# A matrix difference held behind the splits of a three-block sum on VectorE, in the feed-forward of a one-core encoder layer

## The chip, the cores and the metric

The kernel runs on one core of a Trainium2 chip. The metric is the device time of one execution in microseconds (us), the median of the runs. Lower is better.

## The reference

One layer of a hybrid encoder (256 frames, model width 2048, feed-forward width 5632), all in float32. The change lies in the feed-forward; what stands before it (three mixers, gates, an output projection) is left as it is.

```
    h2 = rms_norm(x, g_ffn)
    gate, up = jnp.split(h2 @ w_ffn_in, 2, axis=-1)
    return x + (jax.nn.silu(gate) * up) @ w_ffn_out
```

A final RMSNorm follows. `w_ffn_in` is 2048 x 11264, `w_ffn_out` 5632 x 2048.

## The kernel before, in words

**Products in halves.** TensorE multiplies numbers of a short form (fp32r). So each float32 matrix is split into an upper half (`whi`, ScalarE copies with rounding) and a lower half (`wlo`, VectorE subtracts the upper half from the original), and a product takes three matmul passes: upper by upper, upper by lower, lower by upper. The weights come from memory in float32 and every piece of them, 128 x 1024, is split on the chip: a ScalarE copy (L733) and a VectorE subtraction (L734) for each piece.

**Groups and fewer products.** The gate and up columns are worked off in 22 groups, 256 columns of each per group. A group has four weight blocks of 128 x 2048 (1 MiB each): B11 and B21 (the gate block for the two halves of the model width), X and B22 (the up block likewise). Groups 0 and 1 are plain, with eight block products for a 2 x 2 by 2 x 2 product. Groups 2 to 21 use a scheme with seven products, for which sums of blocks are formed on the chip:

- X arrives as B12 + B22: SyncE loads B12 into X's tile (L765), then a DMA that adds in place, issued by GpSimd (`load_sum`, L769), adds B22 to it.
- `q2` (L877): VectorE adds B11 to X. X is now the three-block sum.
- `q4` (L888): a DMA that adds in place, issued by GpSimd, adds X to B21.
- `q1` (L891): VectorE forms X - B22, which is B11 + B12, into B11's tile. The change is about this difference.

**Pieces.** Every product has two pieces (halves of the block), and the pieces of all groups stand in one list, `line`. In a late group g it reads: X with form 4 (two pieces), a piece of output weights, the sum with form 5 (two), B21 with form 1 (two), output, the difference with form 3 (two), B11 of group g + 1 with form 0 (two), output, B22 with form 6 (two), B21 + X with form 2 (two), output. The output pieces are the second feed-forward matrix for the chunk of groups before it (`down`, 24 matmuls on L115 to L117; a piece of a group has 12, on L792). `run` goes through the list: for each piece it emits the matmuls, and it splits three pieces ahead (`LOOK`), in `split_piece`. A piece has functions to be called before its split (`pre`), after it (`done`) and after its matmuls (`post`). There are four tiles each for upper and lower halves.

**Tiles and loads.** Seven tiles of 1 MiB (`raws`) hold the weights. `Weights` counts the pieces that still use a tile; when the last has been split, the tile goes back and `fill` loads the next block of `todo` into it. `todo` is sorted by the first piece that uses a block (X eight pieces earlier). SyncE issues the plain loads, one after the other: a load that waits for its tile holds up those behind it. GpSimd issues the additions, also in order. Within an engine, the order is set by a scheduler that goes by priorities and dependences; `tc.issue_after` adds a dependence.

**Lines.** The names and lines that matter here: `Piece` (L701), `fill` (L717), `split_piece` (L724), `Group` (L762), `product` (L785), `group` (L874) with `q2`, `q4`, `q1`, and `down` (L938), whose loads are on L945. `turn` (L923) transposes a group's result on TensorE (L931); its four transposes stand behind the sum's product of each group.

Of the kernel before, what the change touches and what calls it, by code (L numbers as in the profile page):

```python
# [7 lines left out]
F32 = mybir.dt.float32  # L8
# [38 lines left out]
def block_kernel(ctx: ExitStack, tc: tile.TileContext, xT, vec,  # L47
                 wvf, wqk, wxy, wpi, wgate, wri, wpool, wbr, wout, wffi, wffo, out):
    nc = tc.nc
    V, S, G, PE = nc.vector, nc.scalar, nc.gpsimd, nc.tensor  # L50
# [8 lines left out]
    class InOrder:  # L59


        def __init__(self, engine):
            self.engine, self.last = engine, None
# [24 lines left out]
    def split(r, a, n, V=V, S=S):  # L88

        hi = hl_p.tile([P, RAW // 2], F32R, name="whi")  # L90
        lo = hl_p.tile([P, RAW // 2], F32R, name="wlo")
        with tc.high_priority(offset=AHEAD):
            S.copy(hi[:, :n], r[:, a:a + n])  # L93
            V.tensor_sub(lo[:, :n], r[:, a:a + n], hi[:, :n].bitcast(F32))  # L94
        return hi, lo
# [207 lines left out]
    def split_w(k):  # L303
        return split(raws[k // 2], k % 2 * W3, W3, Vo, So)
# [14 lines left out]
    for k in range(EARLY):  # L319
# [7 lines left out]
        else:  # L327
            w = split_w(k)
# [13 lines left out]
    w = ahead  # L342
# [12 lines left out]
    for k in range(EARLY, KD):  # L355
# [13 lines left out]
        w = ahead  # L369
# [31 lines left out]
    def scores(h, q, k):  # L401

        sc = aux()
        for t in range(2):
            n = (t + 1) * P
            o = sc[:, off[t]:off[t] + n]
            tq = slice(t * P, (t + 1) * P)
            tl = slice(T + t * P, T + (t + 1) * P)
            PE.matmul(o, lhsT=q[:, tq], rhs=k[:, :n], start=True, stop=False)
            PE.matmul(o, lhsT=q[:, tq], rhs=k[:, T:T + n], start=False, stop=False)  # L410
            PE.matmul(o, lhsT=q[:, tl], rhs=k[:, :n], start=False, stop=False)
            PE.matmul(o, lhsT=LF[:, h, tq], rhs=RF[:, h, :n], start=False, stop=True)
        ns = at_p.tile([P, 3 * P], F32, name="ns")
        st = at_p.tile([P, 8], F32, name="st")
        ph = at_p.tile([P, 3 * P], F32R, name="ph")
        pl = at_p.tile([P, 3 * P], F32R, name="pl")
        for t in range(2):
            c = slice(off[t], off[t] + (t + 1) * P)
            V.tensor_tensor_reduce(out=ns[:, c], in0=sc[:, c], in1=mask[:, c], scale=-1.0,
                                   scalar=3e38, op0=ALU.add, op1=ALU.min, accum_out=st[:, t:t + 1])  # L420
            S.activation(ns[:, c], ns[:, c], AF.Exp, bias=st[:, t:t + 1], scale=-1.0,
                         accum_out=st[:, 2 + t:3 + t])
        V.reciprocal(st[:, 4:6], st[:, 2:4])
        for t in range(2):
            c = slice(off[t], off[t] + (t + 1) * P)
            S.activation(ph[:, c], ns[:, c], AF.Copy, scale=st[:, 4 + t:5 + t])
            V.scalar_tensor_tensor(pl[:, c], ns[:, c], st[:, 4 + t:5 + t], ph[:, c].bitcast(F32),
                                   ALU.mult, ALU.subtract)
        return ph, pl
# [47 lines left out]
    for h in range(H):  # L477
# [3 lines left out]
        p = scores(h, q, k)  # L481
# [157 lines left out]
    for m in range(KD):  # L639
# [3 lines left out]
        for b, y in enumerate((yB, yC, yA)):  # L643
            hi, lo = split(r3, b * 1024, 1024) if b < 2 else split(r1, 0, 1024)
# [56 lines left out]
    class Piece:  # L701
# [3 lines left out]
        def __init__(self, src, mm, uses, pre=(), done=(), post=()):  # L705
            self.src, self.mm, self.uses = src, mm, uses
            self.pre, self.done, self.post = list(pre), list(done), list(post)
            for w in uses:
                w.uses += 1
                if w.first is None:  # L710
                    w.first = len(line)
                    todo.append(w)
            line.append(self)

    line, todo = [], []

    def fill():  # L717

        while raws and todo:
            w = todo.pop(0)  # L720
            w.tile = raws.pop(0)
            w.load(w.tile)

    def split_piece(p, ahead):  # L724
        for f in p.pre:
            f()
        hi = hl_p.tile([P, RAW // 2], F32R, name="whi")[:, :1024]
        lo = hl_p.tile([P, RAW // 2], F32R, name="wlo")[:, :1024]
        w = p.src()
        if len(w.shape) == 3:  # L730
            hi, lo = halves(hi), halves(lo)
        with tc.high_priority(offset=ahead):
            S.copy(hi, w)  # L733
            V.tensor_sub(lo, w, hi.bitcast(F32))  # L734
        for f in p.done:
            f()
        for w in p.uses:
            w.uses -= 1
            if not w.uses:
                raws.append(w.tile)  # L740
        fill()
        p.parts = hi, lo

    def run():

        n = 0
        for i, p in enumerate(line):
            while n < len(line) and n <= i + LOOK:
                split_piece(line[n], AHEAD if n <= LOOK else 0)
                n += 1  # L750
            p.mm(*p.parts)
            for f in p.post:
                f()

    def halves(r):
        return r.rearrange("p (j c) -> p j c", j=2)
# [28 lines left out]
    def product(g, w, form, c, start, pre=None, done=None, post=None, more=()):  # L785

        for h in range(2):
            def mm(hi, lo, h=h):
                o = g.place(c)
                for part, v in ((0, hi), (1, hi), (0, lo)):  # L790
                    for j in range(4):
                        PE.matmul(o, lhsT=hs[:, 4 * h + j, form, part, :], rhs=v[:, :, j * P:(j + 1) * P],  # L792
                                  start=start and h == 0 and part == 0 and v is hi and j == 0,
                                  stop=h == 1 and v is lo and j == 3, skip_group_check=True)

            Piece(lambda h=h: halves(w.tile)[:, :, h * 512:(h + 1) * 512], mm, [w, *more],
                  [pre] if pre and h == 0 else [], [done] if done and h else [],
                  [post] if post and h else [])

    def tmp(nm):  # L800
        return ft_p.tile([P, T], F32, name=nm)

    def gated(t, a, up, g):

        V.scalar_tensor_tensor(a, up, r2[:, t:t + 1], g, ALU.mult, ALU.mult)
# [4 lines left out]
    def first(g):  # L810
        if g.i in PLAIN:
            both(g, g.b11, (("C", 4, True), ("A", 0, True)), lambda: less(g, "t0", "A", "C"))
        else:
            product(g, g.b11, 0, "A", True, post=lambda: copy(g, "m1", "A"))
# [59 lines left out]
    def group(g, nxt, slot, mid):  # L874

        def q2():
            V.tensor_add(g.x.tile, g.x.tile, g.b11.tile)  # L877

        def d():
            g.d = sm.tile([P, T], F32, name="t0")  # L880
            V.tensor_sub(g.d, g.m1, g.bank["B"])

        def silu0():
            g.g0 = sm.tile([P, T], F32, name="t1")
            S.activation(g.g0, g.bank["A"], AF.Silu, scale=r2[:, 0:1])

        def q4():
            G.dma_start(g.b21.tile, g.x.tile, accum_op=ALU.add)  # L888

        def q1():  # L890
            V.tensor_sub(g.b11.tile, g.x.tile, g.b22.tile)  # L891

        def s():
            s_ = sm.tile([P, T], F32, name="evt")
            V.tensor_sub(s_, g.bank["B"], g.m1)
            g.u1 = tmp("u1")
            V.tensor_sub(g.u1, s_, g.bank["C"])

        def up0():
            V.tensor_sub(g.m1, g.bank["B"], g.m1)  # L900
            gated(0, g.m1, g.m1, g.g0)

        def end():
            V.tensor_add(g.d, g.d, g.bank["C"])
            S.activation(g.d, g.d, AF.Silu, scale=r2[:, 1:2])
            gated(1, g.u1, g.u1, g.d)

        product(g, g.x, 4, "C", True)
        slot(0)

        product(g, g.x, 5, "B", True, pre=q2, post=d, more=[g.b11])
        mid()
        product(g, g.b21, 1, "A", False, done=q4, post=silu0, more=[g.x])
        slot(1)
        product(g, g.b11, 3, "B", False, pre=q1, post=s, more=[g.x, g.b22])
        if nxt is not None:
            first(nxt)
        slot(2)
        product(g, g.b22, 6, "B", False, post=up0)
        product(g, g.b21, 2, "C", False, post=end)  # L920
        slot(3)
# [71 lines left out]
    for i, (c, at) in enumerate(owner):  # L993
        g, prev = nxt, (g if i else None)
        nxt = Group(i + 1) if i + 1 < len(owner) else None

        def slot(k):
            if nxt is None and k == 3:
                return
            for _ in range(SLOTS[c][k]):  # L1000
                if queue:
                    queue.pop(0)()

        def mid():
            if prev is None:
                behind(stats)
                return
            pc, pat = owner[i - 1]
            behind(lambda a=(prev, pc, 2 * pat): turn(*a))
            if pc != c:  # L1010
                queue.extend(down(pc))
# [147 lines left out]
```

## Time and profile before

| | |
|---|---|
| median of 3 runs | 1530.01 us (1529.73 to 1530.49) |
| the profiled execution | 1532.99 us, its span 1531.0 us |
| TensorE (PE) busy | 1508.2 us, 99% |
| TensorE weight loads (PEld) busy | 1411.3 us, 92% |
| VectorE (DVE) busy | 1205.4 us, 79% |
| ScalarE (ACT) busy | 923.8 us, 60% |
| GpSimd (POOL) busy | 119.5 us, 8% |
| feed-forward | from about 800 us to the end |

The profile is of one execution. The shares are averages over the whole span, and the stages differ much. Times in the rows are in us from the span's start. A row of the timeline merges neighbouring instructions of one kind: start, length of the stretch, engine, line, operation, out<-in, shape, count, and in brackets the idle time before it and what ended it. An SPq row is a DMA's issue on SyncE; POOL rows with DMA_DIRECT2D are issues on GpSimd. Both say nothing of the landing, which is given apart.

### The profile page before, as it was taken

How to read it: one execution, taken by the hardware profiler on the slowest of the kernel's cores; microseconds unless marked ns; L12 is line 12 of the kernel's file. 1: busy time of each engine (PE TensorE's matmuls, PEld its weight loads, DVE VectorE, ACT ScalarE, POOL GpSimd, SP SyncE). 2: the span in 40 equal slices, each digit the busy share in tenths (PEclk: the TensorE clock that was granted, in tenths of full speed). 3: DMA queues.
4: the chain of work that ended last, by engine and by line, in shares of the span. 5: the costliest groups of instructions: out<-in, count | busy, mean ns of one | idle time of the engine just before them, and what ended most of it. 6: DMA issues, size and time to landing. Idle time of an engine off the chain costs nothing.

```text
span 1531.0 us, 26475 instructions
## 1 busy us (share of the span) xinstructions
PE 1508.2 (99%) x10628; PEld 1411.3 (92%) x10628; DVE 1205.4 (79%) x1593; ACT 923.8 (60%) x1319; POOL 119.5 (8%) x170
## 2 busy tenths in 40 slices
PE   9999999999999999999999999999999999999996
PEld 8988888888888888888889999999999999999996
DVE  7866677788565656567796999999889998999974
ACT  6766567666454444455675666566565665656663
POOL 1000011202000000000110010010000000000012
PEclk9999999999999999999999999999999999999998
DMA  7644455555555554656757699878889888887851
GB/s 259 212 165 150 135 192 185 200 173 206 189 183 199 172 207 165 206 170 234 264 187 219 197 254 277 286 228 252 258 275 295 243 249 267 281 278 242 238 204 55
DMA packets 70858, 331.09 MB, mean 216 GB/s; under 512 B 5584, under 2 KB 6480, under 8 KB 52816
## 3 DMA queue, kind: packets, MB, share of 16 engines
q1 hardware_dynamic: 61840, 286.54, 52.3%
q0 software_dynamic: 8320, 41.95, 14.5%
q8 instruction: 83, 1.36, 0.3%
q10 hardware_dynamic: 576, 0.92, 0.2%
q14 instruction: 39, 0.32, 0.1%
HBM read 306.32 MB, written 2.10 MB: 201 GB/s over the span
## 4 chain that ended last, share of the span: by engine, by line
PE 90%; DVE 4%; DMA 2%; issue 1%; ACT 1%; POOL 0%; SPq 0%; POOLq 0%; DVEq 0%; ACTq 0%
PE acc L106 30%; PE bank L792 23%; PE acc L107 15%; PE obank L117 5%; PE obank L116 5%; PE obank L115 5%; PE bank L834 3%; DVE wlo L734 2%; DMA raw<-raw 2%; PE acc L72 1%; PE aux L72 1%; PE turn L931 1%; DMA raw<-in_wvf 1%; DVE wlo L72 0%; POOL lev L580 0%
## 5 line engine op out<-in xcount | busy, mean ns | idle before, releaser
L733 ACT CAST whi<-raw 128x1024 fp32r<-128x1024 f32 x384 | 393.9, 1050 | 226.9 <-PE obank L116 57.5
L734 DVE TENSOR_TENSOR wlo<-raw,whi 128x1024 fp32r<-128x1024 f32 x384 | 456.4, 1220 | 61.5 <-ACT whi L733 59.0
L106 PE MATMUL acc<-hT,whi 128*128 128x512 f32 x1392 | 489.7, 395 | 0.0
L94 DVE TENSOR_TENSOR wlo<-raw,whi 128x1024 fp32r<-128x1024 f32 (+1 forms) x262 | 320.2, 1222 | 188.9 <-ACT whi L93 188.2
L93 ACT CAST whi<-raw 128x1024 fp32r<-128x1024 f32 (+1 forms) x262 | 270.2, 1032 | 208.5 <-PE acc L106 181.6
L107 PE MATMUL acc<-hT,wlo 128*128 128x256 f32 x1392 | 390.7, 281 | 0.0
L106 PEld LDWEIGHTS acc<-hT,whi 128*128 128x128 f32 x1392 | 261.6, 188 | 59.4
L792 PE MATMUL bank<-whi,hs 128*128 128x256 f32 x2240 | 312.6, 281 | 1.5 <-ACT whi L733 1.5
L792 PEld LDWEIGHTS bank<-whi,hs 128*128 128x128 f32 x2240 | 284.0, 188 | 2.4 <-ACT whi L733 2.1
L107 PEld LDWEIGHTS acc<-hT,wlo 128*128 128x128 f32 x1392 | 262.4, 189 | 0.0
L115 PE MATMUL obank<-act,whi 128*128 128x256 f32 x704 | 197.5, 281 | 0.0
L116 PE MATMUL obank<-act,whi 128*128 128x256 f32 x704 | 197.4, 280 | 0.0
L117 PE MATMUL obank<-act,wlo 128*128 128x256 f32 x704 | 197.3, 281 | 0.0
L792 PE MATMUL bank<-wlo,hs 128*128 128x256 f32 x1120 | 179.1, 282 | 4.6 <-DVE wlo L734 4.4
L792 PEld LDWEIGHTS bank<-wlo,hs 128*128 128x128 f32 x1120 | 151.9, 188 | 7.1 <-DVE wlo L734 6.7
L116 PEld LDWEIGHTS obank<-act,whi 128*128 128x128 f32 x704 | 132.6, 188 | 0.0
L115 PEld LDWEIGHTS obank<-act,whi 128*128 128x128 f32 x704 | 132.4, 188 | 0.0
L117 PEld LDWEIGHTS obank<-act,wlo 128*128 128x128 f32 x704 | 132.3, 188 | 0.1
L106 PE MATMUL acc<-mT,whi 128*128 128x512 f32 x256 | 89.6, 394 | 0.0
L107 PE MATMUL acc<-mT,wlo 128*128 128x256 f32 x256 | 71.5, 280 | 0.0
L769 POOL DMA_DIRECT2D raw<-in_wffi x20 | 24.2, 1210 | 514.7 <-DVE wlo L734 262.6
L106 PEld LDWEIGHTS acc<-mT,whi 128*128 128x128 f32 x256 | 48.1, 188 | 11.2 <-DVE mT L655 0.2
(288 smaller groups left out, 1766.9 us busy)
## 6 DMA issues: line engine op xcount, KB each, us to landing
raw<-in_wffi SPq DMA_DIRECT2D x88, 1024.0 KB, 7.3
raw<-in_wgate SPq DMA_DIRECT2D x48, 1024.0 KB, 4.9
raw<-in_wffo SPq DMA_DIRECT2D x44, 1024.0 KB, 8.6
raw<-in_wffi POOLq DMA_DIRECT2D x20, 1024.0 KB, 8.3
raw<-raw POOLq DMA_DIRECT2D x20, 1024.0 KB, 11.4
raw<-in_wqk SPq DMA_DIRECT2D x16, 1024.0 KB, 4.8
raw<-in_wxy SPq DMA_DIRECT2D x16, 1024.0 KB, 4.9
raw<-in_wbr SPq DMA_DIRECT2D x16, 1024.0 KB, 5.0
```

The lines of the kernel that those rows point to most:

```text
L72: self.last = f(*args, **kw)
L93: S.copy(hi[:, :n], r[:, a:a + n])
L94: V.tensor_sub(lo[:, :n], r[:, a:a + n], hi[:, :n].bitcast(F32))
L106: PE.matmul(ps, lhsT=hi[:, w], rhs=rhs(k), start=first and k == 0, stop=False)
L107: PE.matmul(ps[:, :T], lhsT=lo[:, w], rhs=rhs(k)[:, :T], start=False, stop=last and k == nk - 1)
L115: PE.matmul(o, lhsT=hi[:, w], rhs=rhs(k)[:, :T], start=first and k == 0, stop=False)
L116: PE.matmul(o, lhsT=hi[:, w], rhs=rhs(k)[:, T:], start=False, stop=False)
L117: PE.matmul(o, lhsT=lo[:, w], rhs=rhs(k)[:, :T], start=False, stop=last and k == nk - 1)
L733: S.copy(hi, w)
L734: V.tensor_sub(lo, w, hi.bitcast(F32))
L792: PE.matmul(o, lhsT=hs[:, 4 * h + j, form, part, :], rhs=v[:, :, j * P:(j + 1) * P], start=start and h == 0 and part == 0 and v is hi and ...
L834: PE.matmul(o, lhsT=hs[:, 4 * h + j, form, part, :], rhs=v[:, :, j * P:(j + 1) * P], start=start and h == 0 and part == 0 and v is hi and ...
```

## The change

`q1` moves from the start of the difference's own product (`pre` of form 3) to the end of the sum's splits (`done` of form 5). It is tied by `issue_after` to the second split of the sum, and the first split of B21 is tied to `q1` (through the new field `behind`). B22 is now named among the blocks that the sum's pieces use, and X and B22 are no longer named at the difference's.

```
 class Piece:
     def __init__(self, src, mm, uses, pre=(), done=(), post=()):
         ...
+        self.behind = None
 ...
 def split_piece(p, ahead):
         ...
         with tc.high_priority(offset=ahead):
             S.copy(hi, w)
-            V.tensor_sub(lo, w, hi.bitcast(F32))
+            if p.behind is None:
+                p.sub = V.tensor_sub(lo, w, hi.bitcast(F32))
+            else:
+                with tc.issue_after(p.behind().ins):
+                    p.sub = V.tensor_sub(lo, w, hi.bitcast(F32))
 ...
         def q1():
-            V.tensor_sub(g.b11.tile, g.x.tile, g.b22.tile)
+            with tc.issue_after(g.sums.sub.ins):
+                g.q1 = V.tensor_sub(g.b11.tile, g.x.tile, g.b22.tile)
 ...
-        product(g, g.x, 5, "B", True, pre=q2, post=d, more=[g.b11])
+        product(g, g.x, 5, "B", True, pre=q2, done=q1, post=d, more=[g.b11, g.b22])
+        g.sums = line[-1]
         mid()
         product(g, g.b21, 1, "A", False, done=q4, post=silu0, more=[g.x])
+        line[-2].behind = lambda: g.q1
         slot(1)
-        product(g, g.b11, 3, "B", False, pre=q1, post=s, more=[g.x, g.b22])
+        product(g, g.b11, 3, "B", False, post=s)
```

Two places show what moves. The first is VectorE's order at the three-block sum of group 7. Before, X is in raw23, B11 in raw_8163, B22 in raw_8164, B21 in raw22:

```order
L877 TENSOR_TENSOR raw23_7144<-raw23_7144,raw_8163 128x2048
L956 TENSOR_TENSOR xt_77<-xt_77,obank_10357 128x256
L891 TENSOR_TENSOR raw_8163<-raw23_7144,raw_8164 128x2048
L734 TENSOR_TENSOR wlo_10385<-raw23_7144,whi_10384 128x1024
L734 TENSOR_TENSOR wlo_10402<-raw23_7144,whi_10401 128x1024
L734 TENSOR_TENSOR wlo_10418<-raw22_7143,whi_10417 128x1024
L956 TENSOR_TENSOR xt_77<-xt_77,obank_10421 128x256
L734 TENSOR_TENSOR wlo_10448<-raw22_7143,whi_10447 128x1024
```

After, X is in raw20, B11 in raw_8164, B22 in raw_8165, B21 in raw_8163:

```order
L882 TENSOR_TENSOR raw20_7141<-raw20_7141,raw_8164 128x2048
L964 TENSOR_TENSOR xt_77<-xt_77,obank_10357 128x256
L736 TENSOR_TENSOR wlo_10385<-raw20_7141,whi_10384 128x1024
L736 TENSOR_TENSOR wlo_10402<-raw20_7141,whi_10401 128x1024
L897 TENSOR_TENSOR raw_8164<-raw20_7141,raw_8165 128x2048
L739 TENSOR_TENSOR wlo_10419<-raw_8163,whi_10418 128x1024
L964 TENSOR_TENSOR xt_77<-xt_77,obank_10422 128x256
L736 TENSOR_TENSOR wlo_10449<-raw_8163,whi_10448 128x1024
```

The difference (L891, now L897) stood ahead of the sum's two splits and stands behind them; it is still ahead of B21's two splits.

The second place is SyncE's queue in the same round, from the loads of group 7 to those of group 8. DMASW among a load's waits is the landing of an addition issued by GpSimd. Before (7143 takes B21 of group 7; the load ahead of it, into 7141, is of output weights; behind it come output weights, B22 of group 7, and B11 and X of group 8):

```order
L945 DMA raw21_7142<-in_wffo 128x2x1024 [waits DMAHW5_49,DVE_49]
L765 DMA raw_8164<-in_wffi 128x2x1024 [waits DMAHW6_49,DMAHW4_49,DVE_49]
L765 DMA raw_8165<-in_wffi 128x2x1024 [waits DVE_49]
L765 DMA raw20_7141<-in_wffi 128x2x1024 [waits DMAHW1_49,DVE_49]
L945 DMA raw_8163<-in_wffo 128x2x1024 [waits DMAHW7_49,DVE_49]
L765 DMA raw23_7144<-in_wffi 128x2x1024 [waits DMAHW0_49,DMASW6_49,DMASW3_49]
```

After, in a round of the same pattern (7142 takes B21, 7143 output weights, 7143 later the next X):

```order
L770 DMA raw_8164<-in_wffi 128x2x1024 [waits DMAHW7_49,DVE_49]
L953 DMA raw22_7143<-in_wffo 128x2x1024 [waits DMAHW0_49,DMASW6_49,DMASW3_49]
L770 DMA raw21_7142<-in_wffi 128x2x1024 [waits DMAHW4_49,DMAHW1_49,DVE_49]
L953 DMA raw_8165<-in_wffo 128x2x1024 [waits DVE_49]
L770 DMA raw_8163<-in_wffi 128x2x1024 [waits DMAHW3_49,DVE_49]
L770 DMA raw22_7143<-in_wffi 128x2x1024 [waits DMAHW0_49,DVE_49]
```

Before, the load that waits for the addition is that of B21 (L765), and a load of output weights (L945) stands ahead of it. After, it is a load of output weights (L953), and a block of the group, B22, stands ahead of it. Five loads stand from one such wait to the last load before the next early one in both.

## Rows read from the trace of the kernel before

**Rows 1.** Stages: stretch, its length, busy us of PE, PEld, DVE, ACT, POOL; PEclk, DMA share, GB/s
```profile
900.00:980.00 80.00, 78.49 (x648) 76.82 (x647) 79.72 (x89) 51.37 (x57) 6.28 (x6) 1.00 0.91 260
...
1080.00:1180.00 100.00, 97.99 (x830) 97.57 (x829) 93.12 (x102) 63.65 (x71) 6.31 (x6) 1.00 0.87 272
```

**Rows 2.** Waits of PE, 800 to 1500 us: us in total, times, longest
```profile
PE bank L792 <- DVE wlo L734: 4.4, 6, 1.3
PE bank L792 <- ACT whi L733: 1.5, 3, 0.6
```

**Rows 3.** The chain that ended last, in order of time: start, us, what
```profile
1098.45 12.86 DMA raw<-raw
...
1127.10 2.16 PE bank L792 x16
```

**Rows 4.** Timeline of SyncE's queue: start, us, issue, count
```profile
898.27 21.90 SPq L765 DMA_DIRECT2D raw<-in_wffi  x4
...
981.03 0.37 SPq L765 DMA_DIRECT2D raw<-in_wffi  x1
...
1004.85 0.37 SPq L945 DMA_DIRECT2D raw<-in_wffo  x1
1012.89 0.37 SPq L765 DMA_DIRECT2D raw<-in_wffi  x1
...
1142.39 0.37 SPq L765 DMA_DIRECT2D raw<-in_wffi  x1
...
1173.51 0.37 SPq L765 DMA_DIRECT2D raw<-in_wffi  x1
...
1430.14 0.37 SPq L765 DMA_DIRECT2D raw<-in_wffi  x1
```

**Rows 5.** The same chain, TensorE's part in rounds without a long wait
```profile
1014.09 5.65 PE bank L792 x48
...
1031.45 2.87 PE bank L792 x24
...
1319.40 0.44 PE turn L931 x4
...
1350.81 0.44 PE turn L931 x4
```

**Rows 6.** Timeline of GpSimd: the additions' issues
```profile
915.75 0.89 POOL L888 DMA_DIRECT2D raw<-raw  x1 [6.00 <-DVE wlo L734]
...
1032.63 0.90 POOL L888 DMA_DIRECT2D raw<-raw  x1 [0.49 <-DVE wlo L734]
...
1159.65 1.20 POOL L769 DMA_DIRECT2D raw<-in_wffi  x1 [27.66 <-DVE wlo L734]
```

**Rows 7.** Line L888, its four additions from 860 to 950 us, issue to landing
```profile
DMA to landing us min/median/max: 7.7/7.9/8.0
```

**Rows 8.** Timeline of VectorE in the round of 1012.89
```profile
1015.50 2.35 DVE L734 TENSOR_TENSOR wlo<-raw,whi 128x1024 fp32r<-128x1024 f32 x2
...
1022.63 2.29 DVE L877 TENSOR_TENSOR raw<-raw,raw 128x2048 f32<-128x2048 f32 x1
...
1025.17 2.28 DVE L891 TENSOR_TENSOR raw<-raw,raw 128x2048 f32<-128x2048 f32 x1
1027.37 3.49 DVE L734 TENSOR_TENSOR wlo<-raw,whi 128x1024 fp32r<-128x1024 f32 x3
```

**Rows 9.** Timeline of ScalarE in the same round
```profile
1025.03 2.95 ACT L733 CAST whi<-raw 128x1024 fp32r<-128x1024 f32 x3 [3.30 <-PE bank L792]
```

**Rows 10.** Line L945, the load issued at 1004.85, issue to landing
```profile
DMA to landing us min/median/max: 9.9/9.9/9.9
```

**Rows 11.** Line L765, the load issued at 1012.89, issue to landing
```profile
DMA to landing us min/median/max: 4.9/4.9/4.9
```

**Rows 12.** Line L945, the load issued at 923.49, issue to landing
```profile
DMA to landing us min/median/max: 5.6/5.6/5.6
```

**Rows 13.** SyncE's three loads issued from 1142.39 to 1143.37, issue to landing
```profile
DMA to landing us min/median/max: 5.9/8.0/10.1
```

## Prediction

> **What bounds the kernel now.** I read the stages first. From 900 to 980 us VectorE is busy 79.72 of 80 us and TensorE loses 1.5; from 1080 to 1180 it is 93.12 of 100, TensorE loses 2.0, and the DMA engines are used 0.87 [rows 1]. This is the feed-forward part, the only one that the change touches. The list of waits says what TensorE lacked there: six times the lower half of a split from VectorE, 4.4 us, and three times an upper half from ScalarE, 1.5 us [rows 2]. These 5.9 us are all that TensorE can win, 0.4%.
>
> The chain of waits says what stands behind them. The wait that ends at 1127.10 goes back through a whole round of VectorE work to one DMA of 12.86 us, the addition of X to B21 in place (L888) [rows 3]. I call the landing of that DMA **L**. SyncE's queue shows it in each late round, since the next load into X's tile waits for it: 981.03, 1012.89, 1142.39, 1173.51 and, as the fifteenth, 1430.14 [rows 4]. From the first to the last are 14 rounds, (1430.14 - 981.03) / 14 = 32.08 us each. TensorE alone needs less: with no wait between, its transposes at 1319.40 and 1350.81 are 31.41 us apart [rows 5].
>
> So what takes 32.08? Behind L = 1142.39 SyncE sends five loads; the last is the next X. When it has landed, the addition that completes X (L769) goes out, at 1159.65, 17.3 us after L [rows 6]. The addition to B21 runs behind that one in the same queue, and the next L is 1173.51, 13.9 us later [rows 4]. The round is one of DMAs: 31.1 us here, 32.08 on average. VectorE has slack in it: L888 goes out at 1032.63, 19.7 us after L = 1012.89 [rows 6], and where it stands behind no other addition, in the four early groups, it lands in 7.7 to 8.0 us [rows 7].
>
> **The change, part by part.**
> *Moved on VectorE.* In the round of 1012.89 the sum starts at 1022.63, the difference at 1025.17, the sum's two splits at 1027.37 [rows 8]. The splits no longer wait for the difference: up to 2.2 us sooner. B21's splits stay behind it.
> *Added: an idle stretch.* A split needs ScalarE's copy. That starts at 1025.03, 2.40 us after the sum, three of them in 2.95, so 0.98 each [rows 9]: the first split can start 3.5 us after the sum. VectorE is free after 2.5 (1025.17). It idles 1.0 us that the difference filled.
> *Moved on SyncE.* B22 is now wanted at the sum, and X given up at B21's second half. In the queue, a load of output weights stood ahead of the one that waits for L; now the output weights themselves wait for L, and B22 has the early place. The burst keeps five loads. I take this for the term that decides. Until now the output load went out at 1004.85 [rows 4] and landed 9.9 us later [rows 10], L + 1.9; its first half was split as the second of the pair from 1015.50, done at 1017.85 [rows 8], L + 5.0. Now it goes out at L. The first load behind L took 4.9 us [rows 11]; in the early round of 923.49, where another had gone out 3.7 us before L (898.27 + 21.90 less the issue's 0.37 is 919.80 [rows 4]), it took 5.6 [rows 12]. That is the new order, so I take 5.7. A copy of 1.05, a split of 1.22 and 0.1 between: lower half at L + 8.1, 3.1 us late.
>
> Queued behind it on VectorE are four small operations, X's two splits and the other output half, then the sum: 1022.63 - 1017.85 = 4.8 us without a gap [rows 8]. So the sum starts at L + 12.9 (now 9.7), its first split at + 3.5, L + 16.4 (now 14.5); the second is done at 18.8, the difference at 21.0, B21's splits at 22.2 and, with one small operation between, 23.7. L888 goes out at L + 24.0 (now 19.7).
>
> *Price on TensorE.* It comes to that output piece at 1014.09 + 5.65, L + 6.9 [rows 5], and wants the lower half almost at once: it waits to 8.1. The sum's first half is done at 17.6, near when it is wanted; B21's first half at 22.2 is 1 us late. B21's product ends at L + 24.2, against 1031.45 + 2.87, L + 21.4, now [rows 5]. In all rounds but the last this can go into the round. In the last it is paid: **+3 us**.
>
> *Price on the round.* L888 leaves at L + 24.0 and needs 7.7 to 8.0: 31.8. X's load waits for the other output half, done 0.3 before the sum, L + 12.6; with 4.9 at the least it lands at 17.5, past the 17.3 of L769 now; 0.6 for the hand-over is an estimate, and 13.9 as now: 32.0. TensorE: 31.4. Three chains come within 0.6 us of each other where one led. Bounds: nothing (32.08 stays, the burst hides the delay), and 32.0 - 31.1 = 0.9. I take 0.3, nearer nothing, because in most rounds the burst sets when L769 goes out: 14 x 0.3 = **+4 us**.
>
> *The four early rounds*, 27 us each: L888 queues behind nothing and VectorE is full [rows 1, 7], so the idle 1.0 us counts, less what the vanished waits at the sum give back. I take 0.5 each: **+2 us**, between 0 and 4.
>
> **Sum:** 3 + 4 + 2 = +9 us. The profiled execution took 1532.99 (span 1531.0), 3 us over the median of 1530.01; the terms are differences, so they go on the median: **1539 us**.
>
> A rule that speaks against the change, since B22 is now loaded while L888 flows. The trace first: L888 went out at 915.75 [rows 6], a plain load at 919.80 [rows 4], and it landed within the 7.7 to 8.0 of all four [rows 7], not lengthened. The Trainium skill, DMA: Bandwidth & Descriptors, section Queues, rings and completion order, says that each DMA engine alternates between the queues that have work, a packet from each. By that rule the 3.7 us that L888 has left would be shared and about doubled in each round: 14 x 3.7 = 52 on top, 1591. The trace disagrees.
>
> **Rivals.**
> 1. *Faster, the other side.* The output load lands in 4.9 as at 1012.89, TensorE has by then fallen back far enough not to notice, and the waits at the sum's first half go with the difference. For it: the wait at 1127.10 stands just there. Against it: L sets the round, and the difference is not on the way from L to L. It decides if that load lands before about L + 5. All 5.9 us: 1524; half: 1527.
> 2. *Nothing to measure.* The round of DMAs is as before, and the 3 us at the end are made up by the waits that vanish: 1530, from 1527 to 1533.
> 3. *Worse.* B22's load goes out 3.7 us before L, where the output load had 8.0 (1004.85 to 1012.89), so part of it flows inside the burst. Loads of a burst land at L + 5.9, 8.5 and 11.1 (times to landing 5.9, 8.0, 10.1, issues 0.5 apart [rows 13]), 2.6 apart; half a load is 1.3 us per round, 14 x 1.3 = 18 on top: 1557.
> 4. *Shared queues.* L888 doubled in its last 3.7 us, as above: 1591.
>
> **How the numbers follow.** The forecast, 1533 to 1550 by the bounds of its terms (3; 0 to 13; 0 to 4), has 0.57; rival 1 0.14; rival 2 0.17; rival 3 0.10; rival 4 0.02. A difference under 0.2%, 3.1 us, can't be told from none by a measurement of this kernel. Faster: 0.14. Same: rival 2 and the lowest 0.05 of the forecast, 0.22. Slower: 0.64. The range, 1526 to 1551, takes in the forecast, rival 2 and the nearer part of rivals 1 and 3; about 0.2 lies outside.
>
> **What would show it.** Right: in the late rounds an output load goes out at L and lands 5 to 6 us later; ScalarE waits for that load; TensorE's waits at the sum's first half are gone, and new ones stand at the output piece and at B21's first half; L888 goes out 23 to 24 us after L; rounds of about 32.4. Wrong: rounds of 31.5 with under 3 us of waits on TensorE (rival 1), or rounds over 33 with L769 more than 18.5 us after L (rival 3). If L888 lands within 8 us with B22's load in flight, rival 4 is out.

## Result and profile after

The changed kernel takes **1541.03 us** (median of 3 runs, 1539.70 to 1542.13) against 1530.01: a ratio of 1.0066, 95% interval 1.0049 to 1.0082, so 7.5 to 12.5 us slower. The forecast was 1539, in a range from 1526 to 1551. The profiled execution is the median itself, 1541.03, with a span of 1538.9 against 1531.0: 7.9 us apart. The other 3 us come from the profiled execution of before, which took 1532.99. Wherever a run's granted TensorE clock is on record it was 0.995 to 0.998, but for one run of e12 below (0.584, 2351.45 us), which is left out of its ratio.

Line numbers moved: the split's subtraction is L736 (L739 at B21's first piece, the one tied to the difference), ScalarE's copy L734, the sum L882, the difference L897, B21 += X L893, the addition that completes X L774, SyncE's loads L770 and, for output weights, L953, the products L797, the turn L939.

The stages first, in the columns of [rows 1], which they answer:

```profile
900.00:980.00 80.00, 76.47 (x637) 75.22 (x636) 78.78 (x87) 52.16 (x59) 6.28 (x6) 1.00 0.90 262
1080.00:1180.00 100.00, 100.00 (x851) 100.00 (x850) 93.34 (x103) 63.98 (x70) 6.31 (x6) 1.00 0.89 275
```

In the early stage TensorE loses 3.5 us of 80, where it lost 1.5. The late stretch happens to be one without a loss (100.00), so a longer one is needed. From 985 to 1440 us, before and then after:

```profile
985.00:1440.00 455.00, 450.47 (x3812) 448.97 (x3811) 417.21 (x457) 283.04 (x312) 29.46 (x28) 1.00 0.86 265
```

```profile
985.00:1440.00 455.00, 450.30 (x3773) 446.25 (x3772) 415.56 (x451) 281.42 (x311) 29.46 (x28) 1.00 0.87 263
```

The busy time is the same, 450.47 and 450.30, but 3773 matmuls went through instead of 3812. Busy time can't be trusted here at the per cent; counts and milestones can.

TensorE's waits from 800 to 1520 us (us in total, times, longest), which answer [rows 2]:

```profile
PE bank L797 <- DVE wlo L739: 5.3, 9, 1.0
PE obank L117 <- DVE wlo L736: 2.2, 11, 0.6
PE bank L797 <- ACT whi L734: 1.8, 4, 0.6
```

The waits at the sum's first half (4.4 us in 6) are gone. New ones stand at B21's first half (L739) and at the output piece (L117), the two places that the prediction named; in all 9.3 us instead of 5.9.

SyncE's queue, which answers [rows 4]. Now the load that waits for the landing L is one of output weights (L953):

```profile
984.82 0.37 SPq L953 DMA_DIRECT2D raw<-in_wffo  x1
...
1016.83 0.37 SPq L953 DMA_DIRECT2D raw<-in_wffo  x1
...
1049.08 0.37 SPq L953 DMA_DIRECT2D raw<-in_wffo  x1
...
1434.87 0.37 SPq L953 DMA_DIRECT2D raw<-in_wffo  x1
```

From the first to the last are again 14 rounds: (1434.87 - 984.82) / 14 = 32.15 us each, 32.08 before. The round of L = 1016.83, on VectorE, which answers [rows 8]:

```profile
1023.54 1.23 DVE L736 TENSOR_TENSOR wlo<-raw,whi 128x1024 fp32r<-128x1024 f32 x1 [1.01 <-ACT whi L734]
...
1029.54 2.28 DVE L882 TENSOR_TENSOR raw<-raw,raw 128x2048 f32<-128x2048 f32 x1
...
1033.02 2.36 DVE L736 TENSOR_TENSOR wlo<-raw,whi 128x1024 fp32r<-128x1024 f32 x2 [0.86 <-ACT whi L734]
1035.29 2.29 DVE L897 TENSOR_TENSOR raw<-raw,raw 128x2048 f32<-128x2048 f32 x1
1037.50 1.22 DVE L739 TENSOR_TENSOR wlo<-raw,whi 128x1024 fp32r<-128x1024 f32 x1
1038.63 0.41 DVE L964 TENSOR_TENSOR xt<-xt,obank 128x256 f32<-128x256 f32 x1
1038.96 2.35 DVE L736 TENSOR_TENSOR wlo<-raw,whi 128x1024 fp32r<-128x1024 f32 x2
```

on ScalarE ([rows 9]), and on GpSimd ([rows 6]):

```profile
1022.46 4.11 ACT L734 CAST whi<-raw 128x1024 fp32r<-128x1024 f32 x4 [1.19 <-DMA raw<-in_wffo]
```

```profile
1034.83 1.20 POOL L774 DMA_DIRECT2D raw<-in_wffi  x1 [25.78 <-DMA raw<-in_wffi]
1040.49 0.90 POOL L893 DMA_DIRECT2D raw<-raw  x1 [4.45 <-DVE wlo L736]
```

ScalarE waits 1.19 us for the output load. Line L953, the load issued at 1016.83, issue to landing (before, that load went out 8 us ahead of L and took 9.9, [rows 10]):

```profile
DMA to landing us min/median/max: 5.5/5.5/5.5
```

VectorE waits 1.01 for ScalarE's copy of it, and then 0.86 for the sum's, the idle stretch that the difference used to fill.

TensorE's own milestones are the turns (four transposes for each group, 22 times). The first transposes of the seventh and of the twenty-first turn, before and after:

```profile
999.41 0.27 PE L931 MATMUL turn<-ident,m 128*128 128x128 f32 x1
...
1447.90 0.27 PE L931 MATMUL turn<-ident,m 128*128 128x128 f32 x1
```

```profile
1003.96 0.27 PE L939 MATMUL turn<-ident,m 128*128 128x128 f32 x1
...
1455.73 0.27 PE L939 MATMUL turn<-ident,m 128*128 128x128 f32 x1
```

The second turn starts at 859.81 before and at 860.25 after. So the 7.9 us of the spans are 0.4 ahead of the change, 4.1 from the second to the seventh turn (143.7 instead of 139.6, "early"), 3.3 in the fourteen late rounds (451.8 instead of 448.5) and 0.1 behind them.

### The profile page after: what moved, and what is told of

Same layout as the page of the kernel before. It is cut to its first block, busy times and chain, and to the rows that moved or that the text cites. A ratio compares the mean times of both kernels' runs of the same rounds, so it can differ in the third digit from the quotient of the medians.

```text
span 1538.9 us, 26443 instructions
## 1 busy us (share of the span) xinstructions
PE 1512.6 (98%) x10628; PEld 1412.2 (92%) x10628; DVE 1207.6 (78%) x1593; ACT 923.8 (60%) x1319; POOL 120.4 (8%) x170
## 4 chain that ended last, share of the span: by engine, by line
PE 81%; DVE 10%; issue 4%; DMA 2%; ACT 2%; POOL 0%; SPq 0%; DVEq 0%; POOLq 0%; ACTq 0%
PE acc L106 30%; PE bank L797 17%; PE acc L107 15%; PE obank L117 4%; DVE wlo L736 4%; PE obank L116 4%; PE obank L115 4%; PE bank L839 3%; ACT whi L734 1%; DVE raw L882 1%; DMA raw<-raw 1%; DVE wlo L739 1%; PE acc L72 1%; DMA raw<-in_wffo 1%; PE aux L72 1%
## 5 line engine op out<-in xcount | busy, mean ns | idle before, releaser
L734 ACT CAST whi<-raw 128x1024 fp32r<-128x1024 f32 x384 | 393.5, 1049 | 232.8 <-PE obank L116 84.5
L736 DVE TENSOR_TENSOR wlo<-raw,whi 128x1024 fp32r<-128x1024 f32 x364 | 433.2, 1217 | 60.8 <-ACT whi L734 56.1
L797 PE MATMUL bank<-whi,hs 128*128 128x256 f32 x2240 | 312.9, 281 | 1.8 <-ACT whi L734 1.8
L797 PEld LDWEIGHTS bank<-whi,hs 128*128 128x128 f32 x2240 | 284.2, 188 | 2.6 <-ACT whi L734 2.6
L117 PE MATMUL obank<-act,wlo 128*128 128x256 f32 x704 | 198.3, 282 | 2.2 <-DVE wlo L736 2.2
L797 PE MATMUL bank<-wlo,hs 128*128 128x256 f32 x1120 | 179.9, 282 | 5.5 <-DVE wlo L739 5.3
L797 PEld LDWEIGHTS bank<-wlo,hs 128*128 128x128 f32 x1120 | 151.8, 188 | 8.2 <-DVE wlo L739 7.8
L117 PEld LDWEIGHTS obank<-act,wlo 128*128 128x128 f32 x704 | 132.2, 188 | 4.6 <-DVE wlo L736 4.4
L774 POOL DMA_DIRECT2D raw<-in_wffi x20 | 24.2, 1211 | 476.3 <-DMA raw<-in_wffi 208.0
```

What stands on the lines that cost most here:

```text
L117: PE.matmul(o, lhsT=lo[:, w], rhs=rhs(k)[:, :T], start=False, stop=last and k == nk - 1)
L736: p.sub = V.tensor_sub(lo, w, hi.bitcast(F32))
```

## Experiments

All twelve were timed in 5 rounds beside the kernel before on the same chip. There were four chips, on which before took 1530.6 to 1531.3, so the ratios compare better than the medians. "Early" and "late" are the two stretches above, in each kernel's own trace: one execution each, and that of before ran 3.0 us over its median.

| kernel | median us | ratio to before, 95% | early | late |
|---|---|---|---|---|
| before | 1530.01 | 1 | 139.6 | 448.5 |
| the change | 1541.03 | 1.0066, 1.0049 to 1.0082 | 143.7 | 451.8 |
| e1 place alone | 1531.81 | 1.0005, 0.9996 to 1.0014 | 143.0 | 441.9 |
| e2 loads alone | 1537.59 | 1.0044, 1.0030 to 1.0057 | 140.6 | 452.7 |
| e3 early groups only | 1532.98 | 1.0017, 1.0006 to 1.0028 | 143.3 | 445.8 |
| e4 late groups only | 1537.56 | 1.0041, 1.0028 to 1.0054 | 139.7 | 453.3 |
| e5 place, late groups | 1529.81 | 0.9990, 0.9980 to 1.0001 | 140.1 | 445.6 |
| e6 only B22 early | 1532.64 | 1.0009, 1.0000 to 1.0018 | 142.7 | 444.5 |
| e7 only X early | 1540.39 | 1.0059, 1.0046 to 1.0072 | 143.4 | 449.9 |
| e8 lead for outputs | 1541.72 | 1.0068, 1.0054 to 1.0082 | 142.7 | 451.0 |
| e9 tiles exchanged | 1533.58 | 1.0017, 1.0006 to 1.0028 | 142.3 | 444.6 |
| e10 halves | 1529.75 | 0.9994, 0.9984 to 1.0005 | 140.1 | 446.4 |
| e11 halves, late groups | 1530.06 | 0.9997, 0.9987 to 1.0008 | 139.9 | 446.7 |
| e12 e10, half the output bytes | 1527.19 | 0.9974, 0.9962 to 0.9986 | 139.9 | 441.9 |

**e1 and e2: the two parts apart.** The edits are to the changed kernel. e1 gives back the lists of uses:

```
-        product(g, g.x, 5, "B", True, pre=q2, done=q1, post=d, more=[g.b11, g.b22])
+        product(g, g.x, 5, "B", True, pre=q2, done=q1, post=d, more=[g.b11])
 ...
-        product(g, g.b11, 3, "B", False, post=s)
+        product(g, g.b11, 3, "B", False, post=s, more=[g.x, g.b22])
```

> The difference stays behind the sum's splits on VectorE, but B22 and X are held in the lists of uses as in the kernel before, so SyncE's queue is that of before, row for row. Theory (the loads carry the price: the output weights that wait for L): the output load goes out 8 us ahead of L again, the product of B21 is back at L + 21.4 to 22.4, rounds of 32.1, the end after the last L as before, and only the idle 1.0 us of VectorE in the early rounds is left: 1530 to 1533 us. Rival (the place carries it: B21's splits tied behind the difference, and the idle stretch): 1538 to 1541, with L888's counterpart 1 us or more later after L and the end 3 us longer. A third way, that each half carries its own part: about 1535.

e2 gives back the place, without the two ties:

```
-        product(g, g.x, 5, "B", True, pre=q2, done=q1, post=d, more=[g.b11, g.b22])
+        product(g, g.x, 5, "B", True, pre=lambda: (q2(), q1()), post=d, more=[g.b11, g.b22])
```

> The difference is ahead of the sum's splits again, as before, with B21's splits not tied to it; B22 and X are held as in the change, so SyncE's queue is that of the change, row for row. Theory (the loads carry the price): output load at L, TensorE late at the output piece, B21's product at L + 24, the end 3 us longer: 1537 to 1541 us. Rival (the place carries it): 1530 to 1532. If each half carries its own part: about 1535.

1531.81 and 1537.59: the loads carry most of it, 6.7 us by the ratio, and the place 0.8; the two make 7.5 of 10.1, which their intervals allow. The place alone can't be told from no change, but its trace isn't that of before. In e1 TensorE does not lose anything from 985 to 1440:

```profile
985.00:1440.00 455.00, 455.00 (x3866) 455.00 (x3865) 424.57 (x462) 291.86 (x317) 29.47 (x28) 1.00 0.88 270
```

Its late rounds take 441.9 / 14 = 31.56 us, what TensorE alone needs. (The 31.41 that the prediction gives TensorE is the shorter of two kinds of round that take turns, 31.43 and 31.69 in e1.) Of the 6.6 us that it wins there over the trace of before, 3.4 are paid in the early groups; 1.2 stand ahead of the second turn and 0.6 behind the twenty-first, where the change was at most 0.4 from before. These are its waits from 845 to 985 us, one of 0.9 at most in each of four rounds at the tied split:

```profile
PE bank L797 <- DVE wlo L739: 2.9, 4, 0.9
PE bank L797 <- ACT whi L734: 1.8, 4, 0.6
```

The theory put the end of e1 at that of before, in L's terms; the trace says otherwise: from the last L to the end it has 104.3 us, as the changed kernel has (104.1; before 100.9), yet costs nothing. There L has come forward, TensorE has not gone back.

**e3 and e4: the early and the late groups apart.** The edit is a condition on the group's number around the change's lines: e3 makes the change for groups up to 6, e4 from 7 on (the last group is 21; the texts below count one too few).

> The change in groups 2 to 6 alone, the other fourteen as before. By the profile of the change the early rounds put L at 984.82 instead of 981.03, 3.8 us, the fourteen late rounds 0.9 and the end 3.2. Theory (three separate prices, as forecast): L about 984 to 985 there, then rounds of 32.08 and the end as before: 1533 to 1535 us. Rival (the early shift is taken up by waits later, since a late round is one of transfers that can be shortened): 1530.

> The change in groups 7 to 20 alone. Theory (three separate prices): the first late L at 981.0, then 14 rounds that add 0.9 to 4 us, and 3.2 more behind the last L: 1534 to 1538 us. Rival (what is lost is lost in the early rounds, where VectorE is full): 1530 to 1531. Rival (the end alone): last L at 1430 to 1431 and 1533.

By the ratios 2.6 and 6.3 us, 8.9 together, against 10.1 for the change: within their intervals (2 us or so each way) the prices add up, as forecast. By the turns e3 pays 3.7 early, nearly what the change pays (4.1), and e4 4.8 late. But e3's late rounds are 2.7 shorter than those of before (445.8 and 448.5), which is what its rival said; since the execution of before ran 3.0 us over its median, the two traces can't tell how much of this is real.

**e6, e7, e8, e9: which part of the loads.** e6 and e7 take the uses apart, starting from the change:

```
 e6:
-        product(g, g.b11, 3, "B", False, post=s)
+        product(g, g.b11, 3, "B", False, post=s, more=[g.x])
 e7:
-        product(g, g.x, 5, "B", True, pre=q2, done=q1, post=d, more=[g.b11, g.b22])
+        product(g, g.x, 5, "B", True, pre=q2, done=q1, post=d, more=[g.b11])
 ...
-        product(g, g.b11, 3, "B", False, post=s)
+        product(g, g.b11, 3, "B", False, post=s, more=[g.b22])
```

> The change, but X is held until the difference's splits: B22 alone is loaded early. Theory (the price is the output load that waits for L because B22 took its slot): 1537 to 1541 us, output load out at L as in the change. Rival (the price is X's early release, which moves the queue): 1531 to 1533.

> The change, but B22 is wanted only at the difference's splits, so it is loaded as late as before; X alone is given up early, at B21's second half. Theory (the price is the output load that waits for L because B22 took its slot): 1530 to 1533 us. Rival (X's early release): 1537 to 1541.

Both came out the other way: B22's early load is nearly free (1532.64), X's early release costs all (1540.39). SyncE's queue in one round, in e6 (L = 1111.83) and in e7 (L = 1112.02), shows how:

```profile
1104.69 0.37 SPq L953 DMA_DIRECT2D raw<-in_wffo  x1
1111.83 0.89 SPq L770 DMA_DIRECT2D raw<-in_wffi  x2
```

```profile
1112.02 0.88 SPq L953 DMA_DIRECT2D raw<-in_wffo  x2
```

In the list of loads the output weights stand next after the coming X, and the next tile that is given back is theirs. With X held to the difference's second split, B11's tile is given back ahead of X's, and the output weights get that; it is free 7 us before L. With X released at B21's second split, X's tile is first, and the output weights get the one tile that the in-place addition still reads until L. So the load that decides is as I had it, the output weights behind L; what puts it there is X's release, not B22.

e8 was meant to repair that, with a lead in the list for the output weights, and did not:

```
-            w = Weights(load(m))
+            w = Weights(load(m), 3)
```

> The change as it is, but the output weights get a lead of three places in the list of loads, so that one of them goes out ahead of B22 again. Theory (TensorE is late because the output load waits for L): the waits at the output piece are gone and 1531 to 1535 us. Rival (whatever load waits for L costs the same, B22 as well as the output weights): 1537 to 1541, with the waits now at the difference or at B22's own piece.

Three places don't lift that load over X's in the list. It still gets X's tile; the second output load of the round came forward instead, so that both go out at L (at 1112.15, as in e7). 1541.72 says nothing against the theory, since the edit did not bring an output load out ahead of L, as its text expected. e9 does it from the other side, with a lead for B22:

```
-            self.b22 = Weights(load(1, 1))
+            self.b22 = Weights(load(1, 1), 5 if i not in PLAIN else 0)
```

> The change with B22 and the output weights exchanged in the list of loads (B22 gets a lead of five places), and nothing else: X is still given up early and its tile, which comes free only at L, goes to B22; the output weights get the tile of the difference, free before L. Theory (the whole price of the loads is that the tile which waits for L goes to the output weights, TensorE's first need behind L): 1531 to 1534 us, output load out some 8 us ahead of L, no wait at the output piece, L893's issue at L + 20 to 22. Rival (X's early release costs by itself, whoever gets the tile): 1537 to 1541.

```profile
1104.43 0.37 SPq L953 DMA_DIRECT2D raw<-in_wffo  x1
1110.51 0.88 SPq L770 DMA_DIRECT2D raw<-in_wffi  x2
```

Here X is still released early, but the output load goes out at 1104.43, 6.1 us ahead of L = 1110.51, and B22 takes the tile that waits. 1533.58: of the 0.66% of the change 0.17 are left. The two entries' order in the list is worth 0.49%, 7.5 us.

**e5, e10, e11: can the place win?** e5 is e1 in groups from 7 on, before in the others. (Its text puts what e1 had lost by the turn of 999.4 at 2 to 3 us; by the turns it is 4.5, of which 1.2 stand ahead of the second turn.)

> As e1 (the difference behind the sum's splits, SyncE's queue as in the kernel before), but in groups 7 to 21 alone; groups 2 to 6 as before. In e1's trace the late rounds of TensorE, from turn to turn, are 31.44 and 31.69 us in turn without exception (before 31.4 to 33.1), while up to the turn of 999.4 it had lost 2 to 3 us. Theory (place frees the late rounds from the DMA chain and costs only in the early ones): 1526 to 1528 us, 2 to 4 under before. Rival (the late rounds ran free only because TensorE came to them late): 1530 to 1531, with waits in the late rounds as before.

e10 is e1 with the difference cut in two, e11 the same from group 7 on:

```
+        def q1a():
+            V.tensor_sub(g.b11.tile[:, :1024], g.x.tile[:, :1024], g.b22.tile[:, :1024])
 ...
         def q1():
             with tc.issue_after(g.sums.sub.ins):
-                g.q1 = V.tensor_sub(g.b11.tile, g.x.tile, g.b22.tile)
+                g.q1 = V.tensor_sub(g.b11.tile[:, 1024:], g.x.tile[:, 1024:], g.b22.tile[:, 1024:])
 ...
+        product(g, g.x, 5, "B", True, pre=lambda: (q2(), q1a()), done=q1, post=d, more=[g.b11])
```

> As e1 in all groups, with SyncE's queue as before, but the difference is cut in two halves along the tile: one ahead of the sum's splits, where VectorE otherwise idles 1.0 us for ScalarE's copy, one behind them. Theory (e1 paid about 3 us in the early rounds for that idle time, four waits of 0.9 at B21's first lower half, and ran free afterwards): those waits go, 1528 to 1530 us. Rival (the transfers set the end, what is won early is lost in late rounds again, as in e5): 1530 to 1532.

> The halves of e10 in groups 7 to 21 alone, groups 2 to 6 as before. Theory (VectorE's order sets the late rounds): 1527 to 1529 us, late rounds at 31.44 and 31.69 from turn to turn. Rival (the transfers set them): 1530 to 1531, late rounds as in e5, 31.8 on average.

e10's early waits, to be set against e1's above:

```profile
PE bank L797 <- ACT whi L734: 0.9, 3, 0.4
PE bank L797 <- DVE wlo L739: 0.6, 3, 0.2
```

So the early price is the idle stretch at the sum's copy: filled with half of the difference, it goes from 143.0 to 140.1. But all three end at 1529.8 to 1530.1, and none can be told from before: what is won early comes back in the late rounds, 445.6 to 446.7 instead of e1's 441.9. On the late rounds the rivals of these three texts hold, though e10's 1529.75 by itself lies in its theory's range and the early waits that this theory named are nearly gone. No version up to here is faster than before by more than the measurement can tell.

**e12: what holds the late rounds then.** Every load of output weights brings half of its bytes, so half of the down projection works on old data:

```
             return lambda r: nc.sync.dma_start(
-                r.rearrange("p (m c) -> p m c", m=per),
-                wffo[m:m + per, :, n0 * P:(n0 + n) * P].rearrange("m p c -> p m c"))
+                r[:, :1024].rearrange("p (m c) -> p m c", m=per // 2),
+                wffo[m:m + per // 2, :, n0 * P:(n0 + n) * P].rearrange("m p c -> p m c"))
```

> e10 with half of the bytes: each load of output weights brings only the first half of its tile (the second half of the down projection then works on what an earlier load left there; every instruction of TensorE, VectorE and ScalarE stays). Theory (once TensorE is in time at L, the transfers from L to L set the late rounds, 31.9 us on average in e10 against 31.56 of work): late rounds 31.4 and 31.7 in turn, 1524 to 1526 us. Rival (something on VectorE or ScalarE holds them): as e10, 1529 to 1531, with rounds of 31.9.

The late stretch of e10 and of e12:

```profile
985.00:1440.00 455.00, 453.85 (x3825) 451.49 (x3824) 421.87 (x474) 283.13 (x314) 29.47 (x28) 1.00 0.87 268
```

```profile
985.00:1440.00 455.00, 455.00 (x3865) 455.00 (x3864) 428.47 (x478) 292.01 (x317) 29.46 (x28) 1.00 0.80 233
```

With fewer bytes (a DMA share of 0.80 instead of 0.87) and the same instructions, the late rounds fall from 446.4 to 441.9, TensorE's own time, as e1's. The transfers set the late rounds as soon as TensorE is on time. Whether it is the output loads themselves, now shorter, or the room that they leave to the others, e12 doesn't take apart. The spans differ by 4.6 us (1530.1 and 1525.5), the times by 3.1 by the ratios and 2.6 by the medians: the profiled execution of e10 took 1532.06, above its median. So 1527.19 lies 1.2 us over the theory's range, which was reckoned from that trace. The scatter goes as well: e10's runs lie between 1527.1 and 1533.2, e12's, but for the one named above, between 1526.5 and 1528.4.

## Why the prediction was right, and where not

**The steps of the round hold to 0.3 us.** In the round of L = 1016.83: output load at L, landing after 5.5 (forecast 5.7); its lower half done at 1024.77, L + 7.9 (8.1); sum at 1029.54, L + 12.7 (12.9); its first split at L + 16.2 (16.4); B21's first half done at 1038.72, L + 21.9 (22.2); L893 out at 1040.49, L + 23.7 (24.0); L774 at 1034.83, L + 18.0 (18.1). The durations of before carried over, and the chain of who waits for whom was the right one. Over the fourteen late rounds L893 goes out 23.2 to 25.0 us after L.

**End, +3.** In L's terms right: the last late turn comes 1455.73 - 1434.87 = 20.9 us after L, where it came 1447.90 - 1430.14 = 17.8 after. But e1 shows the same lag and costs nothing, so the lag is a cost only where L has not moved.

**Rounds, +4.** Too large by L in this pair of traces: 14 x 0.07 = 0.9, rounds of 32.15 where about 32.4 were expected. L893 goes out 3.9 us later than before and still keeps the round, because it then lands sooner. Lines L888 and L893, issue to landing, from 1010 to 1440 us, before and after:

```profile
DMA to landing us min/median/max: 10.1/12.1/13.3
```

```profile
DMA to landing us min/median/max: 7.6/8.3/9.4
```

Before, it went out 2.6 us (median) behind the addition to X in the same queue, now 5.7 behind it (1034.83 and 1040.49). That the 4 us were spent standing behind that one is how I read it, and other traces side with it. In e9 it goes out 3.4 us behind, in e2 4.7 (medians); issue to landing in the same stretch, e9 first:

```profile
DMA to landing us min/median/max: 10.1/10.9/11.3
```

```profile
DMA to landing us min/median/max: 8.5/9.7/10.9
```

So in all four kernels it lands some 14.0 to 14.7 us (medians) behind the issue of the addition to X, whenever it went out itself; in e12, with fewer bytes, 15.4. That is near the 13.9 us that the prediction carried over for this stretch. Whether it stands in the queue or shares the engines with that addition no run takes apart. The prediction took the 7.7 to 8.0 of [rows 7] for the end of the new wait, which is why its 32.0 was near: what failed is the difference of 0.3 to a baseline of 32.08 from a single execution, 3.0 us over its median. If those 3 us lie in the late rounds, the +4 holds against the median (0.9 + 3.0); where they lie no run shows.

**Early groups, +2.** The mechanism was right (e10 fills the idle stretch and the price goes), the size was not: 4.1 us by the turns, just past the upper bound of 4. The place alone pays 3.4 of it (e1). The step that failed there is the credit for "what the vanished waits at the sum give back": the early rounds of before had none there, only 1.5 us at ScalarE's copies, which stayed. The rest is a cost that the term left out. From the sixth to the seventh turn the changed kernel takes 36.44 us and e1 35.41: in that round the first output load already waits for L (984.82), and TensorE waits 0.6 us at its piece.

**What decides.** "I take this for the term that decides", of the queue: shown, by e9, 7.5 us. But the sentence named B22's place and X's release together, and only the second counts (e6, e7).

**Rivals.** Faster needed the output load within about 5 us of L; it took 5.1 to 6.8 from the first L to the fifteenth, and TensorE waits. Nothing to measure is out by the interval. Worse needed L774 past L + 18.5 and rounds over 33. L774 came at 18.0 in the round above and at 17.5 to 18.2 in ten of the fourteen. In the other four, from L = 1174.65 on, it came at 18.9 to 19.8, and those rounds took 32.6 to 33.8 us, two of them over 33; there this rival's sign did appear, as in one round of before (19.5, with 34.3). Over all fourteen, 32.15 us on average, it did not. Shared queues needed L893 to lengthen with a load in flight 4 us behind it: it landed in 7.6 to 9.4 in the late rounds, against 7.7 to 8.0 alone [rows 7]. By the rule of the Trainium skill, DMA: Bandwidth & Descriptors, section Queues, rings and completion order, that each DMA engine takes a packet from each queue in turn, its last 3.7 us would double, to some 11.6 by an estimate from that rule and [rows 7]; the trace disagrees for this pair.

**The sum.** +9 against 10.1 by the ratio came out close because an early term that was 2 too small stood beside late terms whose sum, 7, was near what the ratio leaves for them (6.3 in e4, 4.3 to 8.3). How those 7 divide into rounds and end did not come out, so the closeness of the sum is in part luck.

## What to carry to other kernels

Where tiles are handed out from a list, moving the last use of one tile changes who gets which tile. Look up which load inherits the tile that comes free last, and whether it is the one that is needed first; exchanging two entries was worth 7.5 us here, the moved instruction itself 0.8, which can't be told from nothing.

Take losses at the milestones of the engine that binds (here the turns), not as a distance from a transfer: in e1 that distance grew by 3.4 us and no time that could be measured was lost. And where two chains lie within 2% of each other, halve the bytes of one and look whether the other comes free before polishing it.

## What the runs showed of the hardware that was not expected

The same instructions can keep TensorE "busy" for the same time and do less: 3773 matmuls in 450.30 us against 3812 in 450.47. Of some 9.9 us that the changed kernel loses against 31.56 a round in the late stretch, its list of waits there holds 4.5, and all its idle time is 4.7 (455.00 less 450.30). The rest lies inside what counts as busy. Two matmuls of the changed kernel, in a row without a wait, show how:

```profile
1219.78 0.28 PE L115 MATMUL obank<-act,whi 128*128 128x256 f32 x1
1219.89 0.28 PE L116 MATMUL obank<-act,whi 128*128 128x256 f32 x1
```

A record lasts 0.28 us and the next one starts 0.12 later, so up to 0.16 us of each stall is covered by the record before it. Counted from start to start, what goes beyond the usual 0.118 us adds up to 11.9 us in this stretch of the changed kernel and to 1.2 in e1 (starts more than 0.14 us apart).

The first in-place addition of the changed kernel (L893, issued at 862.06) took, from issue to landing,

```profile
DMA to landing us min/median/max: 9.8/9.8/9.8
```

against 7.9 before. It took 9.3 to 10.0 in e1, e3 and e6 to e12, and 7.7 or 7.8 in e2, e4 and e5. The difference's place can't be the cause alone, since e11 leaves that round as before; the cause stays open. It costs e11 next to nothing (early 139.9, before 139.6).
